# The first load of b issued from ScalarE's queue, beside the first load of a on the SP queue

## Chip, cores, metric

One core of one Trainium2 chip. The metric is the device time of one execution in microseconds (us).

## The reference

```python
# a: (16, 512, 512) f32, b: (16, 512, 512) f32
def reference(a, b):
    return np.matmul(a, b.transpose(0, 2, 1)).astype(np.float32)
```

## The kernel before

Batches go in pairs: eight loads of a and eight of b, 2 MB each (two batches, 16 KB to a partition), numbered n = 0 to 15 with a even and b odd, into a ring of NL = 7 buffers. DVE casts a load to bf16 in three copies, TensorE transposes it, ACT (a) and DVE (b) move the transposes out of PSUM, TensorE multiplies, ACT copies the result into one of seven output buffers, and stores of 1 MB go out from POOL (the first eight) and SP (the last eight).

Names: PE is TensorE (matmuls and transposes), DVE VectorE, ACT ScalarE, POOL GpSimd, SP SyncE, which here issues transfers and passes their landings on; a name with q (SPq) is that engine's sequencer. PSUM is the memory into which PE writes. A transfer is cut into packets for 16 DMA engines; each of them raises the transfer's semaphore (a counter on which an engine can wait) when its share is done. A transfer has landed when the last of the 16 has done so. The "go" is the semaphore by which SP lets DVE start on a load.

```python
STORES = "SSSSOSOSOSSOOOOOO"          # POOL: S = store, O = wait for a landing, free a buffer
LATE = {11: (8, 9), 13: (10, 11), 15: (12, 13)}
...
def load(n):
    u, slot = n // 2, n % NL
    src = (a if n % 2 == 0 else b)[2 * u:2 * u + 2].rearrange(
        "e (p j) k -> (e p) j k", j=2 * J)
    if n >= NL:
        nc.sync.wait_ge(s_cd, n - NL + 2)
    nc.sync.dma_start(ld[:, slot], src).then_inc(s_ld[slot], 16)
...
for n in range(NL):
    load(n)
for n in range(2 * pairs):
    nc.sync.wait_ge(s_ld[n % NL], 16 * (n // NL + 1)).then_inc(s_go, 1)   # "go" for DVE, in order
    if n > 0 and n + NL - 1 < 2 * pairs:
        load(n + NL - 1)
    for m in LATE.get(n, ()):
        store(m)
store(batch - 2)
store(batch - 1)
...
nc.gpsimd.wait_ge(s_ld[0], 32)        # POOL's stores start when the eighth load has landed
...
# ACT, first instructions
nc.scalar.nop().then_inc(s_ea, 2)
nc.scalar.nop().then_inc(s_of, NO)
nc.scalar.copy(out=one[:], in_=nc.const_aps.tensor(1.0, (P, 1), f32))   # brings the table load
```

## Time and profile before

| | before |
|---|---|
| time, median of 3 runs (range) | 125.58 us (125.56 to 125.77) |
| span in the profile | 123.9 us |
| bytes moved | 50.33 MB, mean 406 GB/s |
| PE, DVE, ACT busy | 74%, 55%, 55% of the span |
| DMA share, 9 to 114 us | 1.00 |

No engine is busy all the time, but the 16 DMA engines are. A line of the table by stage has: start, end and length of the stretch (us), busy time and number of instructions of PE, PE's weight loads, DVE, ACT and POOL, granted clock of PE, DMA share, GB/s.

### The profile page before, as it was taken

What the parts mean: (1) busy time and instruction counts of PE and PEld (TensorE: products, weight loads), DVE (VectorE), ACT (ScalarE), POOL (GpSimd) and SP (SyncE); (2) the same over time, 40 slices, a digit from 0 to 9 for tenths busy, and PEclk for the clock granted to TensorE, in tenths of its full rate; (3) what the DMA queues carried; (4) which work ended last, traced back from release to release, by engine and by line L of the source; (5) the groups of instructions that cost most, each with busy time, mean ns of one, the idle gap of its engine ahead of it and who ended that gap; (6) DMA issues with size and microseconds to landing.
All of it is one profiled execution on the core that took longest, in us unless ns stands there. A gap on an engine that the chain in (4) does not pass through costs nothing. (4 is left out here: it accounts for less than half of the span.)

```text
span 123.9 us, 2364 instructions
## 1 busy us (share of the span) xinstructions
PE 91.9 (74%) x768; PEld 56.9 (46%) x768; DVE 68.5 (55%) x96; ACT 68.0 (55%) x130; POOL 5.5 (4%) x14
## 2 busy tenths in 40 slices
PE   0005099998999899999989998996699919995000
PEld 0005096457447644764575467444554518441000
DVE  0006596938891897489478658914957068400000
ACT  4002415669558937876595579534956069655000
POOL 2000000000000070001010120000000000000000
PEclk9999999999999999999999999999999986999955
DMA  4999999999999998999999999999999999999980
GB/s 95 397 423 434 428 428 428 423 434 423 428 434 439 439 423 360 439 439 412 436 420 431 450 420 420 431 431 450 410 436 428 410 434 423 423 431 426 434 368 8
DMA packets 4608, 50.33 MB, mean 406 GB/s; under 512 B 512, under 2 KB 512, under 8 KB 512
## 3 DMA queue, kind: packets, MB, share of 16 engines
q1 hardware_dynamic: 3456, 41.94, 80.3%
q0 software_dynamic: 1152, 8.39, 16.0%
HBM read 33.55 MB, written 16.78 MB: 406 GB/s over the span
## 5 line engine op out<-in xcount | busy, mean ns | idle before, releaser
L247 PE MATMUL ps<-tb,ta 128*128 128x512 bf16 x256 | 57.8, 379 | 0.5
L205 ACT COPY ob<-ps 128x512 f32 x64 | 34.4, 589 | 31.1 <-PE ps L247 21.5
L187 ACT COPY ta<-tp 128x512 bf16<-128x512 bf16 x64 | 32.8, 610 | 13.8 <-PE tp L228 13.8
L247 PEld LDWEIGHTS ps<-tb,ta 128*128 128x128 bf16 x256 | 24.1, 97 | 30.6 <-issue 4.0
L228 PE MATMUL tp<-ident,ha 128*128 128x128 bf16 x256 | 20.1, 234 | 14.1 <-PEq L133 14.1
L228 PEld LDWEIGHTS tp<-ident,ha 128*128 128x128 bf16 x256 | 17.0, 105 | 17.9 <-issue 16.0
L168 DVE COPY tb<-tp 128x1024 bf16<-128x1024 bf16 x32 | 21.2, 684 | 4.8 <-DVEq L133 4.8
L228 PE MATMUL tp<-ident,hb 128*128 128x128 bf16 x256 | 18.8, 232 | 6.7 <-PEq L133 6.7
L228 PEld LDWEIGHTS tp<-ident,hb 128*128 128x128 bf16 x256 | 16.6, 105 | 7.2 <-issue 7.2
L152 DVE CAST hb<-ld 128x1024 bf16 x8 | 5.5, 689 | 12.6 <-DVEq L133 12.5
L163 DVE COPY ha<-wa 128x2048 bf16<-128x2048 bf16 x8 | 5.5, 690 | 11.1 <-DVEq L133 11.1
L152 DVE CAST ha<-ld 128x1024 bf16 x8 | 5.6, 705 | 9.8 <-DVEq L133 9.8
L158 DVE CAST wa<-ld 128x2048 bf16 x8 | 9.8, 1220 | 0.0
L158 DVE CAST wb<-ld 128x2048 bf16 x8 | 9.8, 1219 | 0.0
L103 POOL DMA_DIRECT2D out_dram<-ob x8 | 4.8, 607 | 65.5 <-DMA ld<-in_b_dram 41.5
L155 DVE CAST ha<-ld 128x1024 bf16 x8 | 5.6, 700 | 0.0
L167 DVE COPY hb<-wb 128x2048 bf16<-128x2048 bf16 x8 | 5.5, 685 | 0.2
L155 DVE CAST hb<-ld 128x1024 bf16 x8 | 5.5, 686 | 0.0
L178 ACT ACT_TABLE_LOAD x1 | 1.3, 1283 | 1.1 <-SPq L43 1.1
L79 POOL TENSOR_SCALAR_AFFINE_SELECT ident<-ident 128x128 bf16<-128x128 bf16 x1 | 0.3, 284 | 0.2 <-POOL ident L77 0.2
L77 POOL MEMSET ident<- 128x128 bf16 x1 | 0.2, 205 | 0.5 <-SPq L43 0.5
L178 ACT COPY one<-const-float32-1.0 128x1 f32<-128x1 f32 x1 | 0.2, 192 | 0.0
(4 smaller groups left out, 0.4 us busy)
## 6 DMA issues: line engine op xcount, KB each, us to landing
ld<-in_a_dram SPq DMA_DIRECT2D x8, 2048.0 KB, 28.1
ld<-in_b_dram SPq DMA_DIRECT2D x8, 2048.0 KB, 30.4
out_dram<-ob POOLq DMA_DIRECT2D x8, 1024.0 KB, 29.2
out_dram<-ob SPq DMA_DIRECT2D x8, 1024.0 KB, 19.7
```

The source lines that it names most:

```text
L103: engine.dma_start(out[n].rearrange("(p j) n -> p j n", j=J), ob[:, n % NO]).then_inc(s_st[n], 16)
L152: nc.vector.tensor_copy(out=h[:, :J, :], in_=src[:, :J, :HK]).then_inc(s_cd, 1)
L155: nc.vector.tensor_copy(out=h[:, J:, :], in_=src[:, J:, :HK]).then_inc(s_c, 1)
L158: nc.vector.tensor_copy(out=w[:], in_=src[:, :, HK:]).then_inc(s_w, 1)
L163: nc.vector.tensor_copy(out=ha[:], in_=wa[:]).then_inc(s_ca, 1)
L167: nc.vector.tensor_copy(out=hb[:], in_=wb[:]).then_inc(s_cb, 1)
L168: nc.vector.tensor_copy(out=tb[:, ko, :], in_=tp[:, 2 + ko % 2].rearrange("k j p -> k (j p)"),).then_inc(s_eb, 1)
L178: nc.scalar.copy(out=one[:], in_=nc.const_aps.tensor(1.0, (P, 1), f32))
L187: c = nc.scalar.copy(out=ta[:, ko, e * J * P:(e + 1) * J * P].rearrange("k (j p h) -> k j p h", j=J, h=2), in_=tp[:, ko % 2, :, e * HP:(e ...
L205: c = nc.scalar.copy(out=dst[:, j, :].rearrange("m (p j) -> m p j", j=2 * J), in_=ps[:, j, :].rearrange("m (j p) -> m p j", j=2 * J),)
L228: t = nc.tensor.transpose(tp[:, 2 * x + g, j, :], h[:, j, g * P:(g + 1) * P], ident[:])
L247: t = nc.tensor.matmul(ps[:, j, :], ta[:, ko, (e * J + j) * P:(e * J + j + 1) * P], tb[:, ko, :].rearrange("k (j p) -> k j p", j=2 * J)[:, ...
```

## The change

The intent: b's first load should not queue behind SP's issue of a's first load; both go out at once from two queues, so that the first pair has both operands early.

```diff
-        def load(n):
+        def load(n, engine=nc.sync):
...
-            nc.sync.dma_start(ld[:, slot], src).then_inc(s_ld[slot], 16)
+            engine.dma_start(ld[:, slot], src).then_inc(s_ld[slot], 16)
...
-        for n in range(NL):
+        load(0)
+        load(1, nc.scalar)
+        for n in range(2, NL):
             load(n)
```

## The prediction

> **What bounds the kernel now.** I read the page's table of slices first, and in it the two DMA rows:
>
> ```profile
> PE   0005099998999899999989998996699919995000
> DMA  4999999999999998999999999999999999999980
> GB/s 95 397 423 434 428 428 428 423 434 423 428 434 439 439 423 360 439 439 412 436 420 431 450 420 420 431 431 450 410 436 428 410 434 423 423 431 426 434 368 8
> ```
>
> One slice is 123.9/40 = 3.1 us. The DMA engines are 90% busy or more from the second slice to the third from last, at a rate that hardly moves. PE has holes near slices 27 to 30. So I took the table by stage next (columns after the busy times: granted clock, DMA share, GB/s):
>
> ```profile
> 0.00:2.40 2.40, 0.00 (x0) 0.00 (x0) 0.00 (x0) 1.33 (x2) 0.69 (x6) 1.00 0.43 82
> 2.40:9.00 6.60, 0.00 (x0) 0.00 (x0) 0.00 (x0) 0.15 (x1) 0.00 (x0) 1.00 0.91 377
> 9.00:13.80 4.80, 1.87 (x16) 1.63 (x16) 2.44 (x4) 2.05 (x4) 0.00 (x0) 1.00 1.00 430
> 13.80:20.00 6.20, 4.62 (x49) 4.54 (x50) 5.10 (x8) 1.83 (x4) 0.00 (x0) 1.00 1.00 428
> 20.00:43.00 23.00, 21.90 (x195) 13.31 (x193) 17.02 (x25) 16.37 (x33) 0.00 (x0) 1.00 1.01 431
> 43.00:78.00 35.00, 33.35 (x294) 20.23 (x292) 26.20 (x38) 25.48 (x50) 4.83 (x8) 1.00 1.01 425
> 78.00:100.00 22.00, 18.73 (x143) 10.32 (x141) 11.54 (x17) 10.36 (x21) 0.00 (x0) 1.00 1.00 427
> 100.00:114.00 14.00, 11.40 (x80) 6.85 (x80) 6.21 (x9) 10.40 (x20) 0.00 (x0) 0.88 1.01 426
> ```
>
> The DMA share is 1.00 from 9 us to 114 us. The sum closes too: the kernel moves 50.33 MB; at 429 GB/s, the rate at which one 2 MB load follows the other (landings at 9.03, 13.89, 18.78, 23.69 us: 4.89 us each), that is 117.3 us. In the trace's transfer records the first packet starts at 2.38 us, the last of the 16 engines starts at 3.35 us, fifteen engines go quiet near 120.8 to 121.4 us and one at 122.48 us; 3.35 + 117.3 = 120.7. **Bytes bound this kernel**, with about 2.4 us of start before them and about 1.6 us of one straggling engine after them. The timed 125.58 us is the 123.9 us span and 1.7 us outside it.
>
> The chain that ended last is then to be read with care. It shows compute:
>
> ```profile
> 101.68 4.34 PE tp L228 x48
> 107.15 5.57 PE ps L247 x25
> 113.34 0.59 ACT ob L205
> ```
>
> It begins at 101.64 us, after the last load had landed (100.19 us), and the store that it releases at 114.0 us lands at 122.96 us, 9 us later, although 1 MB takes 2.45 us at 429 GB/s. It stood behind earlier stores (landings 115.56, 118.02, 120.48 us). So at the end compute has slack: the DMA engines would reach the last store at about 120.8 - 2.45 = 118.4 us; with 1.4 us from issue to first packet (0.95 to 2.38 us, as at the start) it could be issued as late as about 117.0 us. Slack: 117.0 - 114.0 = 3 us.
>
> **What the Trainium skill says.** "DMA: Bandwidth & Descriptors", section "Issuing engines are not separate DMA queues": transfers from any issuer run on the same 16 engines and interleave, and a second issuer saves only the sequencer's time of issue. Its section "Queues, rings and completion order": an engine goes round robin between the rings that have work, packet by packet. The trace of before agrees where it has two queues: from 48 to 98 us the POOL stores (8 KB packets) get about 145 GB/s and the SP queue (16 KB packets) about 285, one packet each by turns, the sum unchanged. "ScalarE: Activation LUTs", section "What ACT_TABLE_LOAD costs": about 1283 ns; the trace shows 1.28 us.
>
> **The change, part by part.** The start of before, by the timeline:
>
> ```profile
> 0.95 0.38 SPq L95 DMA_DIRECT2D ld<-in_a_dram  x1
> 1.06 1.28 ACT L178 ACT_TABLE_LOAD   x1 [1.06 <-SPq L43]
> 1.38 0.42 SPq L95 DMA_DIRECT2D ld<-in_b_dram  x1
> 9.03 0.69 DVE L152 CAST ha<-ld 128x1024 bf16 x1 [9.03 <-DVEq L133]
> 13.79 0.69 DVE L152 CAST hb<-ld 128x1024 bf16 x1 [2.33 <-DVEq L133]
> 19.94 5.34 PE L247 MATMUL ps<-tb,ta 128*128 128x512 bf16 x23
> ```
>
> (1) Removed: one 0.42 us issue on SP. The five loads behind it are issued 0.4 us earlier. That buys nothing: their data waits behind 2 to 4 MB that are in front of them at the engines.
> (2) Added: one issue of about 0.4 us on ACT at about 1.0 us, ahead of the table load. Table load and the tiny copy end at about 3.0 instead of 2.55 us; ACT's next work is at 11.68 us. Nothing on the path.
> (3) Moved: b's packets now alternate with a's instead of following them. Before, a took all of the rate, landed at 9.03, and b at 13.89. After, with 8 packets of 16 KB per engine in each ring, a ends after about 15 of the 16 packet turns and b after the 16th: b stays at about 13.8 us, a goes from 9.03 to about 13.2 us (13.89 less one packet of 0.611 us). **The first a lands 4.2 us later and b no sooner.** The order on SP (landing of load n raises the go for DVE in order) costs nothing more.
> (4) What that does to the first pair: the casts of a (0.6 + 0.6 + 1.2 us start to start) now begin near 13.2 and end near 15.7; those of b, which began at 13.79, begin near 15.7. That is **about 1.9 us later at the first matmul** (19.94 to about 21.9), not 4.2, since 2.3 us of DVE idling before b goes.
> (5) Whether it reaches the end: pairs are then paced by PE at 11.51 us (the casts to ha start at 21.04, 32.52, 44.03, 55.54, 67.05, 78.56), so the 1.9 us are carried until a load paces again. It does here:
>
> ```profile
> 85.22 0.69 DVE L152 CAST hb<-ld 128x1024 bf16 x1 [4.24 <-DVEq L133]
> 92.80 0.69 DVE L152 CAST ha<-ld 128x1024 bf16 x1 [0.82 <-DVEq L133]
> 100.08 0.69 DVE L152 CAST hb<-ld 128x1024 bf16 x1 [4.86 <-DVEq L133]
> ```
>
> 4.24 us of idling at 85.22 take the 1.9 us up (the b load of the seventh pair lands at 85.33), and 4.86 us at 100.08 take what may be left. Last compute unchanged at about 113.9.
> (6) Whether DMA runs dry meanwhile: before, the eighth load is issued at 14.51 us with five loads (24 us of work) ahead of it; 1.9 us later it still has more than 20. Stores: the first four are released at 43.1 us by the landing of the eighth load, not by compute; the fourth's data is ready at about 39.5, after the change 41.4. Later POOL stores wait for landings of others (55.9, 63.3, 70.7 us). No dry spot, so no byte later.
>
> **Sum:** 0 us on the bytes, 0 on the tail, 1.9 us of compute lost and absorbed. Expected near 125.5 us.
>
> **The rivals.**
> (A) The start gains. The first packets take 0.8 to 1.75 us instead of 0.611, one to an engine (16 in flight at most); a second ring could put a second packet into that latency. At most about 0.8 us per engine, so 124.8 us. For: the DMA share from 2.4 to 9 us is only 0.91. Against: the engines have one packet in flight each, in the steady state too.
> (B) The delay of 1.9 us goes through to the end, or more of it: 127.5 us. It would need the idling of 85 and 100 us to vanish. Against: those waits end on landings which the change doesn't move, and the 3 us of slack behind them. I give it 2%.
> (C) b really starts and lands sooner, since issue was the limit: then the first matmul comes up to 4.9 us earlier, the reading of the change's author. Against: 430 GB/s at share 1.00 between 9 and 13.8 us is the same as in all later stages. Even so the end would not move, for the same reason as in B: about 125.5 us.
> (D) A third ring disturbs the engines: near 46.5 us, where POOL's ring joins, some 16 KB packets take 0.73 to 1.0 us instead of 0.61 and that slice falls to 360 GB/s (some 0.5 us lost: 3.1 x 70/430). The same at the start would give 126.1 us.
>
> **Range and chances.** A and D are of like size and opposite; the gain seems slightly likelier, so 125.4 us. Before's runs spread 0.2 us. With A at its full 0.8 and D at 0.5: 124.8 to 126.1 us. 2% is 2.5 us, more than any rival but B gives in full: same 0.97, faster 0.015, slower 0.015.
>
> **What would show it right or wrong.** Right: the first a cast at 13 to 13.5 us instead of 9.03; the first b cast at about 15.7; first matmul near 21.9; the DMA share from 13.8 us still 1.00; the idle time before the hb cast near 85 us smaller by about 2 us; last compute ending near 114; last landing within 0.5 us of 122.96. Wrong: a landing still near 9 (no alternation; then nothing moves at all), a DMA share below 1.00 anywhere between 14 and 114 us, or a last store issued after 117 us. A time below 124.8 or above 126.1 us would mean that the start of the transfers, or the straggling engine at the end, depends on the rings in a way that I don't see.

One correction before it is used. The landings and first packets in it, which come from the trace's transfer records and not from a view, stand on a time axis that runs 0.43 us late against the views: landings of the first loads are 8.60, 13.46, 18.35 us (not 9.03, 13.89, 18.78), the first packet is at 1.95 us, the last landing at 122.52 us. Differences between two of them hold. Those between one of them and a time of a view are 0.43 us too long: from SP's first issue to the first packet it is 1.0 us and not 1.4 (0.95 to 1.95 us), and the b load that seems to land at 85.33, after its own cast (85.22), landed at 84.89. The slack of 3 us is not touched, since both of its ends are shifted. From here on all times are on the views' axis. The 0.43 us from landing (8.60) to cast (9.03) are the way over SP's wait and the go for DVE, which the prediction's two equal numbers hid.

## The result

| | before | changed |
|---|---|---|
| time, median of 6 runs (range) | 125.60 us (125.56 to 126.03) | 125.53 us (125.30 to 125.80) |
| ratio, 95% interval | | 0.9989 (0.9970 to 1.0007): the same |
| first b landed / first a landed | 13.46 / 8.60 us | 12.89 / 13.06 us |
| last landing | 122.52 us | 122.26 us |

The timeline of the changed kernel at the start (start, length, engine and line, operation; its lines after 95 are numbered two higher than before):

```profile
0.91 0.39 ACTq L95 DMA_DIRECT2D ld<-in_b_dram  x1
0.95 0.86 SPq L95 DMA_DIRECT2D ld<-in_a_dram  x2
1.48 1.28 ACT L180 ACT_TABLE_LOAD   x1 [1.48 <-SPq L43]
13.50 0.69 DVE L154 CAST ha<-ld 128x1024 bf16 x1 [13.50 <-DVEq L135]
15.84 0.69 DVE L154 CAST hb<-ld 128x1024 bf16 x1
21.40 3.83 PE L249 MATMUL ps<-tb,ta 128*128 128x512 bf16 x16
```

b is issued 0.47 us earlier, the table load moves from 1.06 to 1.48 us, and the first cast of a moves from 9.03 to 13.50 us. The first 512-wide matmul comes 1.46 us later. The casts that wait for late loads, from DVE's timeline:

```profile
84.89 0.69 DVE L154 CAST hb<-ld 128x1024 bf16 x1 [2.45 <-DVEq L135]
92.53 0.69 DVE L154 CAST ha<-ld 128x1024 bf16 x1 [0.83 <-DVEq L135]
99.82 0.69 DVE L154 CAST hb<-ld 128x1024 bf16 x1 [4.86 <-DVEq L135]
```

The idle time at 85 us has shrunk from 4.24 to 2.45 us: the late start is paid there, and the casts after it come 0.3 us earlier than before in this profile, as the loads do (in the second profile, below, 0.02 to 0.06 us). The table by stage (granted clock, DMA share and GB/s at the end) and the slices:

```profile
2.40:9.00 6.60, 0.00 (x0) 0.00 (x0) 0.00 (x0) 0.55 (x2) 0.00 (x0) 1.00 0.96 402
9.00:13.80 4.80, 0.00 (x0) 0.00 (x0) 0.30 (x1) 0.00 (x0) 0.00 (x0) 1.00 1.01 430
43.00:78.00 35.00, 33.27 (x295) 20.41 (x296) 25.88 (x38) 25.47 (x50) 4.09 (x8) 1.00 1.00 419
```

```profile
DMA  4999999999999999999999999999999999999990
GB/s 148 413 435 429 429 429 424 429 424 435 435 424 424 429 392 363 445 416 424 453 405 437 443 408 443 424 424 458 397 445 427 408 429 427 429 427 429 424 387 8
```

The stage from 2.4 to 9 us moves 402 GB/s instead of 377: a small gain at the start, which the prediction held as a rival. The stage from 43 to 78 us moves 419 instead of 425: in this profile part of it is gone again there. The chain that ended last has the same pieces, 0.26 us earlier:

```profile
106.89 5.57 PE ps L249 x25
113.08 0.59 ACT ob L207
```

### The profile page after: what moved, and what is told of

Its sections match the earlier page's. It is cut to its first block, busy times and chain, and to the rows that moved or that the text cites. A ratio compares the mean times of both kernels' runs of the same rounds, so it can differ in the third digit from the quotient of the medians.

```text
span 123.7 us, 2364 instructions
## 1 busy us (share of the span) xinstructions
PE 90.8 (73%) x768; PEld 55.9 (45%) x768; DVE 68.1 (55%) x96; ACT 68.0 (55%) x130; POOL 5.2 (4%) x14
## 5 line engine op out<-in xcount | busy, mean ns | idle before, releaser
L230 PE MATMUL tp<-ident,ha 128*128 128x128 bf16 x256 | 19.3, 228 | 18.1 <-PEq L135 18.1
L230 PEld LDWEIGHTS tp<-ident,ha 128*128 128x128 bf16 x256 | 16.3, 102 | 21.9 <-issue 20.1
```

Of the source, the lines that this page charges most:

```text
L230: t = nc.tensor.transpose(tp[:, 2 * x + g, j, :], h[:, j, g * P:(g + 1) * P], ident[:])
```

## Experiments

Theory: bytes bound the kernel, and a delay of compute at the start is absorbed, up to a limit, by the waits for late loads and by the queue ahead of the last store. Rivals: the chain of compute is the bound and the gain and loss happen to cancel; two queues start the transfers quicker (rival A of the prediction). Each experiment starts from the kernel before or the changed one; each was timed beside runs of the kernel before on the same chip.

### Again, in more rounds

No edit.

> The changed kernel itself, timed in more rounds, to settle what the first comparison left open (0.9989, interval 0.997 to 1.0007). Theory G (the start of the transfers gains about 0.55 us because all 16 engines have work at 2.3 us; most of it is given back when the POOL stores join at 43 to 50 us): ratio 0.997 to 0.999, first a cast at 13.5, the eighth load landed near 42.3 instead of 42.8, the last landing 0.2 to 0.3 us earlier than in the kernel before. Rival N (nothing but noise between runs): ratio 1.000 within 0.001 and the eighth load's landing scattered about 42.8.

Measured: 125.54 us (5 runs), before 125.80 us (11 runs), ratio 0.9981 (0.9964 to 0.9998). The eighth load landed at 42.52 us (before: 42.83), the last landing was at 122.31 us (before: 122.52). The last store was issued at 114.10 us here, 0.15 us later than in the kernel before, where the first profile had it 0.26 us earlier. The direction of the time is theory G's, the size some 0.2 us, at the edge of what is resolved; the rival is not ruled out, since hold1, below, shows as much without the cause.

### hold1: the delay alone

```diff
         for n in range(2 * pairs):
+            if n == 0:
+                nc.sync.wait_ge(s_ld[1], 16)
             nc.sync.wait_ge(s_ld[n % NL], 16 * (n // NL + 1)).then_inc(s_go, 1)
```

> The kernel before with all loads on SP, but the first go for DVE held until b has landed too: the compute delay of the change without its second ring. Theory (compute's delay is absorbed by the waits for late loads): first a cast near 13.9, first 512-wide matmul near 21.8, the idle time before the hb cast near 85 us smaller by about 2 us, time as before within 0.2 us (125.4 to 125.8), eighth load landed at 42.8. Rival B (a delay at the start goes through to the end): 127.4 us.

Measured: 125.63 us, ratio 0.9988 (0.9972 to 1.0004). First cast at 14.02, first 512-wide matmul at 22.27 us, 2.3 us later than before; idle time before the b cast near 85 us 1.79 us instead of 4.24:

```profile
85.11 0.69 DVE L154 CAST hb<-ld 128x1024 bf16 x1 [1.79 <-DVEq L135]
```

Eighth load at 42.98 us. The delay that the change brings is worth nothing by itself, so nothing that the second queue gives had to make up for it. The ratio is also the changed kernel's first ratio to four digits: a reminder of how little 0.1% says here. The last store was issued 0.79 us later than before, though the last b cast began at 100.01 us (before: 100.08). By the trace's clock records PE ran at half clock from 103.32 to 106.73 us, where before it did so from 101.26 to 104.67 us, and its last two groups of transposes took 1.99 and 1.82 us instead of 1.70 and 1.06. It is not the hold that does this alone: in pause (below), which holds nothing back, the stretch was 102.93 to 106.34 us and the last store was issued at 114.60.

### hold3 and hold4: how much delay is absorbed

The same edit with `s_ld[3]` and `s_ld[4]`.

> The kernel before, first go held until the fourth load has landed (23.3 us): casts start near 23.8, first 512-wide matmul near 31.7, 11.8 us later than before. Theory (a delay is absorbed by the waits for late loads, 9.9 us of DVE idling, and then by 3 us of slack of the last store): pairs paced by PE at 11.51 us put the last pair's b casts near 104.2 instead of 100.1 and the last store's issue near 118 instead of 114, which is 1.1 us past the slack: time 126.7, range 125.9 to 127.6. Rival B (a delay goes through): 137 us. If slack is larger than I think: 125.6.

> The same, held until the fifth load (28.2 us): casts near 28.6, first 512-wide matmul near 36.5, 16.6 us later than before. Theory: the slack is spent, each further us counts: last compute near 122.6, time 130 (129 to 132). If instead the DMA engines run dry where the stores join at 43 us, since their data is then not ready, it shows as a dip of GB/s there and a longer time, up to 134.

Measured: 127.76 us, ratio 1.0176 (1.0153 to 1.0199), and 132.63 us, 1.0564 (1.0547 to 1.0581). Both lie above their expected ranges, though the time does turn up where a finite tolerance wants it, and not at the rival's 137. The table by stage of the first one's end (PE busy in the first column after the length; DMA share and GB/s last):

```profile
108.00:112.00 4.00, 3.51 (x59) 3.22 (x58) 2.49 (x4) 4.00 (x9) 0.00 (x0) 1.00 1.01 424
112.00:116.00 4.00, 3.94 (x26) 1.84 (x24) 1.29 (x2) 2.11 (x5) 0.00 (x0) 1.00 0.84 352
116.00:120.00 4.00, 3.64 (x17) 1.47 (x15) 0.00 (x0) 2.71 (x6) 0.00 (x0) 1.00 0.25 106
120.00:124.00 4.00, 0.00 (x0) 0.00 (x0) 0.00 (x0) 0.42 (x1) 0.00 (x0) 0.77 1.03 426
```

Here the DMA engines wait for compute: from 116 to 120 us they are a quarter busy while PE works, and only then move the last stores. The last store was issued at 120.45 us, 6.5 us later than before, where I had expected about 4. My sum was wrong: I had added up DVE's idling (9.9 us), but part of that idling lies beside PE's work on the pair before and could never be saved. The right measure is PE's: paced by PE alone, the kernel takes 88.7 us from the first 512-wide matmul (31.78) to the last store's issue (120.45). From 19.94 us that would end at 108.6; it ended at 113.95, so 5.3 us are absorbed by waits for loads (and by the stretch of half clock that follows the last of them in the kernel before; hold3 has none there). With nothing ahead of it but the store before, the last store lands 4.2 us after its issue (120.45 to 124.62), so the last one may be issued at 122.5 - 4.2 = 118.3 us, 4.3 us later than before. Together 9.6 us of tolerance. hold4's first matmul is 16.5 us late: 6.9 us too much, and it lost 7.0 us. No dip at 43 us in either (413 and 401 GB/s at the lowest between 40 and 52 us).

### hold2: the tolerance, tested

The same edit with `s_ld[2]`.

> The kernel before, first go held until the third load has landed. From the two longer holds: compute paced by PE alone takes 88.6 us from the first 512-wide matmul to the last store's issue (31.78 to 120.42), so the first matmul at 19.94 would end at 108.6 were it not for late loads, and 114.0 - 108.6 = 5.4 us are absorbed there; a store that finds the engines idle lands 4.2 us after its issue, so the last may be issued at 122.5 - 4.2 = 118.3, 4.3 us more. Tolerance 9.7 us. This hold puts the first 512-wide matmul near 27.0, 7.1 us late: last store issued near 115.7, time as before (125.4 to 125.8). If the tolerance is only the 5.4 us of the waits for loads, it is 127.3 us.

Measured: 125.90 us against 125.80 us, ratio 1.0011 (0.9992 to 1.0030). First 512-wide matmul at 26.85 us, 6.9 us late; last store issued at 115.54, 1.6 us later than before; last landing 122.55 us. More delay than the waits for loads can absorb, and still no loss, because the last store stands in a queue. This is the one test of the sum that was made ahead of its result; the sum itself is hold3's, and hold4, with which it agrees, was known when it was made. hold2 shows a tolerance of at least 6.9 us; the 9.6 us rest on hold3 and hold4.

| kernel | first 512-wide matmul | later by | last store issued | last landing | ratio |
|---|---|---|---|---|---|
| before | 19.94 us | 0 | 113.95 us | 122.52 us | 1 |
| changed | 21.40 | 1.5 | 113.69 | 122.26 | 0.9989, 0.9981 |
| hold1 | 22.27 | 2.3 | 114.74 | 122.47 | 0.9988 |
| hold2 | 26.85 | 6.9 | 115.54 | 122.55 | 1.0011 |
| hold3 | 31.78 | 11.8 | 120.45 | 124.62 | 1.0176 |
| hold4 | 36.48 | 16.5 | 125.14 | 129.30 | 1.0564 |

### less1: fewer bytes

```diff
+            if n == 8:
+                nc.sync.dma_start(ld[:, slot, :J], src[:, :J]).then_inc(s_ld[slot], 16)
+                return
             nc.sync.dma_start(ld[:, slot], src).then_inc(s_ld[slot], 16)
```

> Wrong on purpose: the kernel before with 1 MB of 50.33 MB left out (the ninth load brings half of its rows), nothing else changed. If bytes bound the kernel, the time falls by 1.049 MB / 429 GB/s = 2.45 us: 123.1 us, ratio 0.980; later loads land 2.4 us earlier and the last store is issued near 111.6. If the chain of compute that the profile shows as ending last were the bound by itself, the time would stay at 125.6.

Measured (wrong results, as meant): 123.31 us against 125.80, ratio 0.9809 (0.9787 to 0.9832), 2.4 us less by the ratio; the last landing is at 120.08 us, 2.44 us earlier. Its table by stage:

```profile
43.00:78.00 35.00, 33.34 (x299) 20.44 (x297) 25.68 (x37) 25.46 (x50) 5.53 (x8) 1.00 1.01 425
100.00:114.00 14.00, 10.62 (x64) 6.26 (x64) 2.82 (x5) 9.29 (x18) 0.00 (x0) 0.88 1.01 427
```

These are the same rates as before (425 and 426), with less to move; compute did all that it did before, on some stale rows. Two expectations were missed: the last two loads landed 3.6 and 3.7 us earlier, not 2.4, and the last store was issued at 113.41 us, only 0.5 us earlier, not near 111.6. That makes the reading stronger: the chain of compute ended 0.5 us earlier, the last landing came 2.44 us earlier, as the bytes want it. With hold1 and hold2 this settles the bound: 1 MB less is worth its 2.4 us, 6.9 us of delay are worth nothing that these runs resolve.

### a_on_act and split: is it the second queue that starts quicker?

```diff
-        load(0)
-        load(1, nc.scalar)
-        for n in range(2, NL):
+        load(0, nc.scalar)
+        for n in range(1, NL):
             load(n)
```

> Mirror of the change: the first a goes from ScalarE's queue, b and all others from SP. If the quicker start of the transfers belongs to having two rings, or to ScalarE's ring, the first 16 packets start within 0.35 us of each other and the eighth load lands near 42.3, as in the changed kernel; if it belongs to tensor b's data being read first, the start is as in the kernel before (5 of 16 engines late, eighth load at 42.8). Casts of a near 13.4 either way; time 125.3 to 125.7.

```diff
+            if n == 0:
+                for h, engine in enumerate((nc.sync, nc.scalar)):
+                    part = slice(h * J, (h + 1) * J)
+                    engine.dma_start(ld[:, slot, part], src[:, part]).then_inc(s_ld[slot], 16)
+                return
```

(The waits on this buffer's count are raised by 16.)

> The first a in two halves of 1 MB, one from SP and one from ScalarE, then b and the rest from SP: two rings at the start and nothing put beside a. Theory: a lands near 8.1 to 8.6 (first cast 8.5 to 9.0) so compute is not delayed, and the start of the transfers gains as in the changed kernel (eighth load near 42.3); the end moves by the gain that is left, 0 to 0.4 us: 125.2 to 125.6. Rival C (an earlier first pair is worth its own length): no more than that either since compute starts no earlier than 0.5 us before.

Measured: a_on_act 125.55 us, ratio 0.9980 (0.9961 to 0.9999); split 125.61 us, ratio 0.9992 (0.9975 to 1.0009). By the transfer records, bytes moved by 14 us: changed 4.80 and 4.75 MB (second profile), a_on_act 4.73; before 4.55, split 4.55, and between 4.51 and 4.64 in the other kernels that start on SP alone. So it is not b's data that starts quicker: with a on ScalarE's queue the gain is much the same. It takes two whole loads on two queues; two halves of one load bring no bytes, and a no sooner than SP alone does (halves landed at 8.45 and 8.90 us, before 8.60; I had expected 8.1 to 8.6). The first 16 packets had started by 2.55 us in a_on_act (0.61 us after the first, not within 0.35 as expected), by 2.25 in the changed kernel, by 2.92 in the before kernel. The eighth load landed at 42.84 us in a_on_act, not near 42.3 as I had expected; only the engine that finishes a load first was early (41.82, against 42.12 before). That holds for every kernel: where two whole loads start on two queues, the first engine is done with the eighth load at 41.77, 41.78 and 41.82 us, in all ten other kernels between 42.03 and 42.37; so the gain at the start is still there at 42 us. In split a is within 0.3 us of before, b at 13.63 us (before 13.46), and the time is the same as with the change, where a is 4.5 us later. It does not test rival C, since no kernel here starts the first pair earlier.

### pause: do SP's own next issues slow the start?

```diff
-        for n in range(NL):
+        load(0)
+        nc.sync.wait_ge(s_set, 2)
+        for n in range(1, NL):
             load(n)
```

> The kernel before, but SP waits for the identity matrix (1.7 us) before its second load. If the late start of some engines (two near 2.9 us, where most start by 2.2) comes from SP's next issues coming right behind the first, all 16 start by 2.3 us and the first packets take less than 1.1 us; if it comes from there being one ring only, or from the first reads of HBM, the start is as in the kernel before. Time not distinguishable from before.

125.69 us. Some engines still got their first packet only near 3.0 us, and 4.54 MB had moved by 14 us, as before. But the wait moved the second issue only from 1.38 to 1.70 us, still ahead of the first packet (1.98 us), so this does not clear SP's next issue. What the late engines come from stays open.

### nopool: stores without POOL

```diff
-    STORES = "SSSSOSOSOSSOOOOOO"
-    LATE = {11: (8, 9), 13: (10, 11), 15: (12, 13)}
+    STORES = "OOOOOOOOO"
+    LATE = {5: (0, 1), 7: (2, 3), 9: (4, 5), 11: (6, 7), 13: (8, 9), 15: (10, 11, 12, 13)}
```

> The kernel before with all 16 stores on SP's queue, each pair of stores behind a load whose landing comes after its data, and none on POOL. Theory (bytes and one straggling engine set the end; the straggler's lag of 0.7 us in the load phase grows to 1.2 to 1.8 us while POOL's stores run): the spread of landings stays near 0.7 us, no dip of GB/s near 46 us, last landing 121.0 to 121.6 instead of 122.5: time 124.2 to 124.8, ratio 0.989 to 0.994. Rival (the straggler is there whoever issues): 125.6. Risk: stores wait longer in SP's ring, output buffers come free late and compute stalls, up to 127.

Measured: 130.25 us, ratio 1.0357 (1.0324 to 1.0390). The named risk came true, and went beyond the 127 us named. From the timelines of ACT and of PE:

```profile
65.58 2.05 ACT L205 COPY ob<-ps 128x512 f32 x4 [6.65 <-ACTq L133]
68.75 1.99 PE L228 MATMUL tp<-ident,ha 128*128 128x128 bf16 x16 [5.37 <-PEq L133]
```

ACT waits 6.65 us for an output buffer whose store (landed at 65.25 us) stood behind loads in SP's queue, and PE after it. But the theory failed too: with no transfer of POOL's at all, the landings of one store by the 16 engines lay up to 2.8 us apart at the end (115.77 to 118.58 us). It is not the same picture, though: in the kernel before, the last of the 16 landings of the store before the last comes 1.21 us after the one before it (117.59, 116.38 us), so one engine lags; in nopool that step is 0.62 us, and several engines are spread out. So landings drift apart without POOL; whether the single lagging engine is POOL's doing stays open. Where the DMA engines had been idle just before, as for the last store of hold3 and hold4, the 16 landings lie only 0.15 and 0.17 us apart: the lag is there only after the engines were kept busy.

### tail15: which engine lags

```diff
+            if n == batch - 1:
+                dst = out[n].rearrange("(p j) n -> p j n", j=J)
+                for lo, hi in ((0, 120), (120, 128)):
+                    engine.dma_start(dst[lo:hi], ob[lo:hi, n % NO]).then_inc(s_st[n], 16)
+                return
```

(The wait for this landing is 32.)

> The kernel before, the last store cut in two: partitions 0 to 119 (which 15 engines can share) and 120 to 127. In the kernel before one engine ends 1.3 us after the others. If it is the one that serves the last share of partitions and is left out of the large part, the last landing comes about 1 us earlier: 124.4 to 124.8 us. If it is another, each engine has up to two packets of 0.31 us more: 125.6 to 126.2.

Measured: 126.16 us, ratio 1.0033 (1.0016 to 1.0050), last landing 122.93 us. The second reading: the engine that lags was not relieved. The last two landings of the two pieces came at 122.63 and 122.93 us, 0.30 us apart, and the third last at 121.83. One 8 KB packet takes 0.31 us, so this fits one engine that served both pieces, the small one last. The records do not name it. What makes it lag stays open, and so does the 1.3 us at the end that it costs.

## Why the prediction was right

**Bound by bytes:** right, shown by less1 and the hold series. The DMA share stayed at 1.00 from 9 to 114 us.

**(1), (2) issues:** right. ACT's issue took 0.39 us at 0.91 us, the table load ended at 2.76 us, ACT's next work was at 16.14 us.

**(3) alternation:** the size was right, the order wrong. The first a was to be cast at 13 to 13.5 us and was at 13.50. But I had a finish first and b stay at 13.8; b's packets came first (first ones 1.93 to 2.25 us, those of a 2.67 to 3.39). ACT issued 0.04 us before SP; in a_on_act it did so too, and again its load (there a) came first. Whether the 0.04 us decide it or the queue does was not tested. b landed at 12.89 us, 0.57 us sooner than before, a at 13.06. The Trainium skill says in "DMA: Bandwidth & Descriptors" ("Issuing engines are not separate DMA queues") that transfers from different issuers run on the same 16 engines and interleave. The trace agrees, and shows what follows for two equal loads: they finish together, 0.17 us apart.

**(4) 1.9 us at the first matmul:** the b cast came at 15.84 us as predicted (15.7), the first 512-wide matmul only 1.46 us later. The rest is TensorE's speed. From PE's timeline, three of the four groups of 16 transposes, before:

```profile
15.38 1.86 PE L228 MATMUL tp<-ident,hb 128*128 128x128 bf16 x16 [2.89 <-PEq L133]
17.12 1.87 PE L228 MATMUL tp<-ident,ha 128*128 128x128 bf16 x16
18.78 1.33 PE L228 MATMUL tp<-ident,hb 128*128 128x128 bf16 x16
```

and changed:

```profile
17.43 1.83 PE L230 MATMUL tp<-ident,hb 128*128 128x128 bf16 x16 [0.47 <-PEq L135]
19.16 1.05 PE L230 MATMUL tp<-ident,ha 128*128 128x128 bf16 x16
20.51 1.05 PE L230 MATMUL tp<-ident,hb 128*128 128x128 bf16 x16 [0.29 <-PEq L135]
```

A group takes 1.87 us or 1.05 us. The Trainium skill, "TensorE: Matmul & The Clock Gate" (Part 1), says that the array runs at half clock until it has been busy for some 3.4 us. Before, 2.89 us of idling lay between the first two groups; changed, 0.47 us, and the third group was already fast. In hold1, with the same 0.47 us, it was not:

```profile
19.69 1.85 PE L230 MATMUL tp<-ident,ha 128*128 128x128 bf16 x16
```

That it is the clock, the trace's own clock records show: the full clock is on record from 19.34 us before, from 19.09 changed and from 21.40 in hold1, and the groups turn fast just there. (The table by stage says 1.00 for earlier stages only because it counts a time without a record as full.) When it comes is less regular than a fixed 3.4 us: 4.0 us after the first transposes changed (15.09 to 19.09 us), 4.5 in the changed kernel's second profile, where the third group took 1.24 us and the first 512-wide matmul came at 21.68, 1.74 us later than before, and 5.8 in hold1. So the 0.5 us by which the matmul came sooner than predicted hang on where the switch fell, and are luck. I had priced the transposes as equal.

**(5) absorption:** right in its place and result. The idling near 85 us fell from 4.24 to 2.45 us, and the last compute ended 0.26 us earlier than before (0.15 us later in the second profile). Wrong in its limit, which the prediction did not need: counting DVE's idling promises 9 us of absorption where PE's pace leaves 5.3. The slack behind it, which I put at 3 us, comes out at 4.3 from hold3; the likely reason is that I priced the last store at the engines' mean and not by the one that lags.

**(6) no dry spot:** right, even with 16.5 us of delay no dip came where the stores join.

**The rivals:** A happened at the start, and its counter-argument (one packet in flight to an engine anyway) failed. The gain lay in the first 16 packets: they started at 2.08 us on average instead of 2.24 and took 0.91 us instead of 1.30 (second profile 2.06 and 1.13, a_on_act 2.14 and 1.07; kernels that start on SP alone 2.18 to 2.30 and 1.20 to 1.39). So engines began sooner, and their first packets were shorter too; why is not shown. Two loads on two queues had 0.18 to 0.25 MB more moved by 14 us than the kernel before, 0.4 to 0.6 us of work at 429 GB/s. By 100 us that lead is lost in the scatter: 41.53, 41.58 and 41.60 MB with two whole loads on two queues, 41.45 in the kernel before, but 41.56 in hold1 and 41.53 in hold2, which start on SP alone. Where it goes differs from profile to profile: between 43 and 50 us, where POOL's stores join, the changed kernel moved 2.74 MB in one profile and 2.97 in the other, the kernel before 2.89. The last landing was 0.08 to 0.26 us earlier than before in these three profiles; in split, which had moved no more bytes by 14 us, it was 0.23 us earlier (122.29). About 0.2 us is the size of the run-to-run spread; the timed ratios (0.9989, 0.9981, 0.9980) lean that way, and hold1's 0.9988, without any such start, leans as far. Whether anything is gained stays open below 0.4%. B is out by hold1 and hold2. C did not happen: b landed only 0.57 us sooner, and the first matmul came later. D's loss at the start did not come: after it the rate was 430.

## What to carry to other kernels

Where the DMA engines are busy throughout, as here, look at which load is needed first before giving two loads a queue each: sharing the engines they finished together, b at 12.89 us (before 13.46) and a at 13.06 (before 8.60), so the one needed first was delayed. Before trying to start compute earlier, find out what a start is worth: hold it back by one, two, three loads and see where the time begins to rise. And count slack on the engine that paces (here PE from the first matmul, and the queue ahead of the last store), not by adding up idle times of an engine that waits on it.

## What the Trainium skill lacked or had wrong

- "DMA: Bandwidth & Descriptors", "Latency and other measured facts": it gives about 0.6 us to the first byte from SP or ACT, without saying from when. Here the first packet came 1.0 us after SP's issue began and 0.62 us after it ended (1.33 to 1.95 us), so it agrees if it counts from the end. But the sixteenth packet started only 0.97 us after the first, and these 16 took 0.61 to 1.75 us, 1.30 on average, where most later ones take 0.61. The page has no word on this slow start.
- Same page, "Issuing engines are not separate DMA queues": it says that a second issuer saves only sequencer time. That agrees within the timing here, but with two full loads on two queues 0.18 to 0.25 MB more than in the kernel before had moved by 14 us, and with one load cut into two halves none.
- Same page, same table as the first point, the row on slower engines: it gives, as a best guess, contention that only POOL-issued transfers have. Here landings of one store spread by 2.8 us with no POOL-issued transfer in the kernel (nopool), so engines drift apart without it. Whether the one engine that ends 1.24 us after the others in the kernel before is one of the two that the row names, the records don't say, so the guess is neither borne out nor refuted.
- No page that I found has the whole way from a landing over SP's wait and a second semaphore to the first cast: 0.43 us (8.60 to 9.03 us).
